# Strict triangle and partial products of a triangular substitution held in PSUM, corner products on other PSUM banks

## The chip, the core and the metric

The kernel runs on one core of a Trainium2 chip, in one launch. The metric is the device time of one execution in microseconds (us). The kernel before has a median of 1243.59 us over three runs (1241.88 to 1249.92). Engine names are those of the profile: PE is the matrix engine (PEld its weight loads), DVE the vector engine, ACT the scalar engine, POOL the GpSimd engine, SP the engine that issues most DMAs. SBUF is the large on-chip memory; PSUM is the small one that PE writes, eight banks of 512 float32 numbers in each of 128 partitions.

## The reference

256 tokens of width 1024 pass through a block of attention, retention, cross attention and a mixture of experts, and then through a second block of two layers. The second layer of that block opens with a "time mix" of 16 heads of width 64, and only its recurrence concerns the change:

```
def _rwkv7_step(state, inp):
    r_t, w_t, k_t, v_t, a_t, b_t = inp
    sa = jnp.einsum('bhvk,bhk->bhv', state, a_t)
    state = (state * w_t[:, :, None, :] + sa[..., None] * b_t[:, :, None, :]
             + v_t[..., None] * k_t[:, :, None, :])
    return state, jnp.einsum('bhvk,bhk->bhv', state, r_t)
```

Each head's state takes a rank-one correction in every one of the 256 steps. The result then passes a group norm, a gate and the product with `w_o`, and a feed-forward part ends the layer.

## The kernel before

The kernel goes through the phases A to G in turn. Phase F is the time mix (`phase_f`), G the feed-forward part behind it. The code is written in one order; a scheduler sets, engine by engine, the order in which the instructions stand, and each engine then works its queue strictly in that order, waiting on semaphores.

Phase F cuts the 256 steps into four chunks of 64. Inside a chunk the corrections form a unit lower triangular system for each head, and the kernel inverts it. 4 chunks x 16 heads give 64 triangles of 64 x 64. Each is split into two diagonal triangles of 32 x 32 and a corner. The 128 small triangles lie one to a partition.

- **The triangles.** PE forms the products `ar` x `kb`; ACT copies the diagonal blocks into the tile `Lc`; DVE transposes `Lc` into `Ll` (L1757), after which each partition holds one strict triangle as 32 x 32 numbers.
- **The substitution.** A loop of 31 steps (L1758 in the source; its instructions are recorded under the helper line L329): step `s` multiplies column `s` of `Ll` below the diagonal by row `s` of the growing inverse `Xl` into a temporary tile from the ring `s` (seven buffers in this phase), and adds that to `Xl`. That is 62 DVE instructions of (31-s)(s+1) elements each, every one dependent on the one in front of it.
- **Beside it.** The table `BETWEEN["substitution"]` names the steps that are written next to the loop, in order: `v` (second half of the value projection), `c` (`corners`: PE forms the corner products, ACT copies them to `Lo`), `p` (`products`: the 128 x 128 products of chunks 0 to 3; ACT copies them into the tiles `G`, called `k` in the trace, and POOL masks them, L1786), `g` (`gate`, whose second operand POOL splits, L364), `t` (`turned`: PE transposes keys into `BK`).
- **PSUM.** Two pools of four banks each: `psa` (tiles `acc`) and `psb` (tiles `ps`). The value projection, `products`, `turned` and `gate` take `acc`; the triangles, `corners` and the steps behind the substitution take `ps`.
- **Behind it.** DVE transposes `Xl` back into `XC` (the buffer `Lc`, L1839) and into `YC` (L1840). `merge` computes the corner of the inverse on PE in two rounds with DVE copies between them (`P1`, then `X`); ACT copies the diagonal parts from `Lc` into `X`.
- **POOL.** It multiplies the values by `bon` into the tiles `gb` (L1886, eight instructions; `gb` is allocated from the ring `s`), fetches `rowF` in four DMAs (L1894), clears `R` (L1889), and later folds the gate into `gb` and `gt`.
- **The chunk loop.** For each chunk, PE forms `pr`, ACT copies it to `R` (L1943), PE multiplies `R` by `X` (`ps<-R,X`), ACT copies the result to `UV` (L1950), and PE forms outputs and the new state. `normed` runs the group norm: 16 ACT instructions `s<-acc,gnb,gr` for the first two chunks. `lin_res` multiplies by `w_o`, part of which lies split in `held`.

Of the kernel before, what the change touches and what calls it, by code (L numbers as in the profile page):

```python
# [15 lines left out]
ALU = mybir.AluOpType  # L16
# [3 lines left out]
P = 128  # L20
# [189 lines left out]
class Block:  # L210
# [1249 lines left out]
    def phase_f(self, x, with_ffn):  # L1460
        nc = self.nc
# [25 lines left out]
        for b in range(4):  # L1487
# [6 lines left out]
            s = slice(2 * b, 2 * b + 2)  # L1494
# [61 lines left out]
        pr = [self.psa(512) for _ in range(4)]  # L1556
# [171 lines left out]
        def run(spec):  # L1728
            for k in spec:
                next(steps[k], None)  # L1730
# [6 lines left out]
        Lc, Lo, Ll, Xl = (k32(n) for n in ("Lc", "Lo", "Ll", "Xl"))  # L1737
# [6 lines left out]
        for p in range(2):  # L1744
            pl = [self.psb(512).rearrange("p (n x) -> p n x", n=8) for _ in range(2)]
# [4 lines left out]
            for hh in range(2):  # L1750
# [3 lines left out]
                        self.act(Lc[r, 16 * p + hh : 16 * p + 16 : 2, :], pl[hh][r, :, 32 * b : 32 * b + 32])  # L1754
                run(BETWEEN["removals"][2 * p + hh])

        nc.vector.transpose(Ll, Lc.rearrange("p n t -> p t n"))  # L1757
        for s in range(31):  # L1758
            n, m = 31 - s, s + 1
            pr = self.s2(n * m).rearrange("p (a b) -> p a b", a=n)  # L1760
            self.tt(pr, Ll[:, m:, s : s + 1].broadcast_to([P, n, m]), Xl[:, s : s + 1, 0:m].broadcast_to([P, n, m]), ALU.mult)
            self.tt(Xl[:, m:, 0:m], Xl[:, m:, 0:m], pr, ALU.add)

        G = []
# [52 lines left out]
                    yield  # L1817

        def corners():
            pl = [self.psb(512).rearrange("p (n s) -> p n s", n=16) for _ in range(2)]  # L1820
            r = [slice(Us(q).start + 32, Us(q).start + 64) for q in range(2)]
            for p in range(2):
                for i in range(8):
                    for q in range(2):
                        for ps, rh in zip(pl, halves):
                            self.mm(ps[r[q], 8 * p + i, :], ar[rh, i, 2 * p + q, 0, 32:64], bT(rh, i, 2 * p + q)[:, 0:32], True, True)
            for hh in range(2):
                for q in range(2):
                    self.act(Lo[r[q], hh::2, :], pl[hh][r[q]])
            yield  # L1830

        steps["c"] = corners()
        steps["p"] = chain.from_iterable(products(c) for c in range(4))
        steps["t"] = chain.from_iterable(turned(c) for c in range(3))
# [74 lines left out]
        pr, pu = [self.psb(512) for _ in range(2)], [self.psb(512) for _ in range(2)]  # L1909
# [26 lines left out]
        for c in range(4):  # L1936
            p, q = c // 2, c % 2
# [230 lines left out]
```

## Time and profile before

| | |
|---|---|
| median of three runs | 1243.59 us |
| the profiled execution | 1244.74 us |
| its span, first to last instruction | 1242.9 us |
| busy share of the span: PE, DVE, ACT, POOL | 90%, 58%, 46%, 17% |
| mean granted TensorE clock | 0.957 |
| span part in which phase F's substitution stands | about 914 to 964 us |

The profile is one execution recorded by the hardware. A timeline row gives the start in us from the span's start, the duration, engine, line, operation, what it writes and reads by tile name (buffer numbers left out), a count, and in brackets how long the engine stood idle before it and on whom. Rows of one kind may be merged, and their duration is then that of the stretch. [...] Busy shares over the whole span mix stages with different limits, so a stage is read from its own stretch.

### The profile page before, as it was taken

How to read it: one execution, taken by the hardware profiler on the slowest of the kernel's cores; microseconds unless marked ns; L12 is line 12 of the kernel's file. 1: busy time of each engine (PE TensorE's matmuls, PEld its weight loads, DVE VectorE, ACT ScalarE, POOL GpSimd, SP SyncE). 2: the span in 40 equal slices, each digit the busy share in tenths (PEclk: the TensorE clock that was granted, in tenths of full speed). 3: DMA queues.
4: the chain of work that ended last, by engine and by line, in shares of the span. 5: the costliest groups of instructions: out<-in, count | busy, mean ns of one | idle time of the engine just before them, and what ended most of it. 6: DMA issues, size and time to landing. Idle time of an engine off the chain costs nothing. (4 is left out here: it accounts for less than half of the span.)

```text
span 1242.9 us, 18727 instructions
## 1 busy us (share of the span) xinstructions
PE 1121.5 (90%) x7070; PEld 869.8 (70%) x7070; DVE 725.4 (58%) x1332; ACT 574.0 (46%) x1114; POOL 217.3 (17%) x192
## 2 busy tenths in 40 slices
PE   6999999979888868999999999579993988999998
PEld 5778878734333316878888887578972977888887
DVE  4978565531111106765766665986679646766665
ACT  5667555310000005675545544457772344555452
POOL 2101000000000011200000000786575820100000
PEclk9999999979999979999999999897997798999999
DMA  8543595899999985633766664133411205766662
GB/s 279 169 118 116 177 395 189 296 349 409 409 409 409 409 346 174 170 119 119 223 186 188 192 192 127 40 84 103 151 41 35 69 18 169 214 190 190 187 187 68
DMA packets 125154, 246.04 MB, mean 198 GB/s; under 512 B 11666, under 2 KB 66354, under 8 KB 125059
## 3 DMA queue, kind: packets, MB, share of 16 engines
q1 hardware_dynamic: 123250, 240.52, 57.8%
q0 software_dynamic: 1520, 4.01, 1.1%
q8 instruction: 57, 0.93, 0.3%
q10 hardware_dynamic: 288, 0.26, 0.1%
q14 instruction: 39, 0.31, 0.1%
HBM read 243.70 MB, written 1.05 MB: 197 GB/s over the span
## 5 line engine op out<-in xcount | busy, mean ns | idle before, releaser
L364 DVE TENSOR_TENSOR ws<-w,ws 128x1024 fp32r<-128x1024 f32 (+5 forms) x341 | 327.1, 973 | 161.9 <-ACT ws L363 161.0
L363 ACT CAST ws<-w 128x1024 fp32r<-128x1024 f32 (+6 forms) x365 | 288.3, 805 | 219.3 <-issue 83.3
L312 PE MATMUL ps<-fp,ws 128*128 128x512 f32 (+1 forms) x1472 | 253.8, 333 | 0.2
L312 PEld LDWEIGHTS ps<-fp,ws 128*128 128x128 f32 x1472 | 220.7, 189 | 31.3 <-DVE fp L187 0.6
L312 PE MATMUL acc<-ws,f 128*128 128x512 f32 (+1 forms) x696 | 175.2, 404 | 11.9 <-ACT ws L363 9.3
L312 PEld LDWEIGHTS acc<-ws,f 128*128 128x128 f32 x696 | 131.2, 193 | 41.3 <-ACT ws L363 11.3
L326 ACT ACTIVATE s<-ps 128x256 f32<-128x256 f32 (+2 forms) x114 | 47.0, 414 | 220.7 <-PE ps L312 220.6
L312 PE MATMUL acc<-ws,h 128*128 128x512 f32 x528 | 124.1, 391 | 0.0
L312 PEld LDWEIGHTS acc<-ws,h 128*128 128x128 f32 x528 | 97.7, 188 | 21.0
L312 PE MATMUL acc<-f,ws 128*128 128x256 f32 x480 | 69.9, 301 | 18.2 <-DVE ws L364 11.4
L312 PE MATMUL ps<-we,xs 128*32 128x512 f32 x512 | 76.7, 605 | 3.2 <-DMA we<-in_experts_dram 1.8
L312 PEld LDWEIGHTS acc<-f,ws 128*128 128x128 f32 x480 | 64.5, 204 | 21.3 <-DVE ws L364 13.3
L347 POOL TENSOR_TENSOR rs_r<-rs_v,mhalf 128x2 f32<-128x2 f32 (+3 forms) x26 | 24.4, 944 | 298.6 <-DVE kan L338 180.3
L1112 DVE TENSOR_TENSOR xs<-ps,cols 128x256 f32<-128x256 f32 x32 | 13.6, 424 | 101.8 <-PE ps L312 101.7
L312 PE MATMUL acc<-ws,o 128*128 128x512 f32 x192 | 48.0, 405 | 1.3 <-ACT ws L363 1.2
L312 PEld LDWEIGHTS ps<-Pm,x 128*128 128x128 f32 x256 | 31.9, 198 | 23.1 <-issue 18.8
L312 PE MATMUL acc<-ws,mf 128*128 128x512 f32 x192 | 48.0, 399 | 0.0
L329 DVE TENSOR_TENSOR s<-ps,s 128x256 f32<-128x256 f32 x80 | 33.5, 420 | 24.8 <-ACT s L326 24.8
L312 PE MATMUL ps<-we,hT 128*32 128x512 f32 x256 | 38.6, 663 | 10.2 <-DMA rowD<-in_rowD_dram 6.6
L312 PEld LDWEIGHTS ps<-we,xs 128*32 128x32 f32 x512 | 15.6, 109 | 41.4 <-issue 26.9
L312 PEld LDWEIGHTS acc<-ws,o 128*128 128x128 f32 x192 | 36.4, 194 | 10.0 <-ACT ws L363 1.6
L312 PEld LDWEIGHTS acc<-ws,mf 128*128 128x128 f32 x192 | 35.2, 188 | 6.9
(405 smaller groups left out, 1470.7 us busy)
## 6 DMA issues: line engine op xcount, KB each, us to landing
we<-in_experts_dram SPq DMA_DIRECT2D x192, 512.0 KB, 10.2
w<-in_ffn_w_gate_dram SPq DMA_DIRECT2D x44, 512.0 KB, 4.4
w<-in_ffn_w_up_dram SPq DMA_DIRECT2D x44, 512.0 KB, 4.0
w<-in_ffn_w_down_dram SPq DMA_DIRECT2D x44, 512.0 KB, 3.7
w<-in_hy_w_in_dram SPq DMA_DIRECT2D x20, 512.0 KB, 3.9
w<-in_w_in_dram SPq DMA_DIRECT2D x16, 512.0 KB, 4.5
w<-in_cross_w_kv_dram SPq DMA_DIRECT2D x16, 512.0 KB, 4.1
w<-in_rw_w_o_dram SPq DMA_DIRECT2D x10, 512.0 KB, 3.6
```

Of the source, the lines that this page charges most:

```text
L312: return self.nc.tensor.matmul(out, lhsT, rhs, start=start, stop=stop, skip_group_check=True)
L326: self.nc.scalar.activation(out, in_, func, **kw)
L329: self.nc.vector.tensor_tensor(out, a, b, op)
L347: self.rooted = self.nc.gpsimd.tensor_tensor(r, v, self.mhalf[:, :n], ALU.pow).ins
L363: i = self.nc.scalar.copy(a, src)
L364: j = (sub or self.nc.vector).tensor_tensor(b, src, a.bitcast(F32), ALU.subtract)
L1112: return nc.vector.tensor_tensor(xs[:, 2 * b : 2 * b + 2, :], ps.rearrange("p (k c) -> p k c", k=2), gb, ALU.mult)
```

## The change

The strict triangle is copied after the transpose from `Ll` into two PSUM tiles `Lp` (ACT, 128 x 512 each: columns 0 to 15 and 16 to 31), and the loop reads it there. The products go to one PSUM tile `pr2`, to its two halves in turn, and no longer to the ring `s`. Every instruction of the loop then has one operand in SBUF and one in PSUM. The three tiles come from `psb`; `corners` takes its two banks from `psa` in exchange. The arithmetic is the same.

```
         nc.vector.transpose(Ll, Lc.rearrange("p n t -> p t n"))
+        Lp = [self.psb(512).rearrange("p (t s) -> p t s", t=32) for _ in range(2)]
+        for h in range(2):
+            nc.scalar.copy(Lp[h], Ll[:, :, 16 * h : 16 * h + 16])
+        pr2 = self.psb(512)
         for s in range(31):
             n, m = 31 - s, s + 1
-            pr = self.s2(n * m).rearrange("p (a b) -> p a b", a=n)
-            self.tt(pr, Ll[:, m:, s : s + 1].broadcast_to([P, n, m]), Xl[:, s : s + 1, 0:m].broadcast_to([P, n, m]), ALU.mult)
+            at = s % 2 * 256
+            pr = pr2[:, at : at + n * m].rearrange("p (a b) -> p a b", a=n)
+            self.tt(pr, Lp[s // 16][:, m:, s % 16 : s % 16 + 1].broadcast_to([P, n, m]), Xl[:, s : s + 1, 0:m].broadcast_to([P, n, m]), ALU.mult)
             self.tt(Xl[:, m:, 0:m], Xl[:, m:, 0:m], pr, ALU.add)
...
         def corners():
-            pl = [self.psb(512).rearrange("p (n s) -> p n s", n=16) for _ in range(2)]
+            pl = [self.psa(512).rearrange("p (n s) -> p n s", n=16) for _ in range(2)]
```

The scheduler then sets other orders from this place to the end of phase F. Lines behind the loop move down by six (L1786 becomes L1792, L1886 L1892, L1889 L1895).

**POOL, beside the substitution.** Before: the splits of the gate's operand (`ws`), the masks of chunk 0 (`k_1963`) and chunk 1 (`k_1990`), splits of `w_o`, and only then the eight `bon` products into `gb`.

```order
L364 TENSOR_TENSOR ws_8557<-w_8550,ws_8556 128x512
L364 TENSOR_TENSOR ws_8563<-w_8560,ws_8562 32x512
L1786 TENSOR_TENSOR k_1963_8526<-k_1963_8526,c_gmask 64x16x64
L1786 TENSOR_TENSOR k_1963_8526<-k_1963_8526,c_gmask 128x16x64
L364 TENSOR_TENSOR ws_8567<-w_8560,ws_8566 32x512
L1786 TENSOR_TENSOR k_1990_8632<-k_1990_8632,c_gmask 64x16x64
L1786 TENSOR_TENSOR k_1990_8632<-k_1990_8632,c_gmask 128x16x64
L364 TENSOR_TENSOR ws_9498<-w_9495,ws_9497 128x512
L364 TENSOR_TENSOR ws_9502<-w_9495,ws_9501 128x512
L1886 TENSOR_TENSOR s_2013_8878<-k_1786_7619,bon 64x512 x2
```

In the changed kernel two `bon` products already stand further up, and the other six and three DMAs stand ahead of the gate's last splits and of the mask of chunk 0 (`k_1935`):

```order
L364 TENSOR_TENSOR ws_8531<-w_8524,ws_8530 128x512
L1892 TENSOR_TENSOR s_1986_8853<-k_1786_7619,bon 64x512
L1892 TENSOR_TENSOR s_1987_8854<-UV_7620,bon 64x512
L1892 TENSOR_TENSOR s_1987_8854<-UV_7621,bon 64x512
L1892 TENSOR_TENSOR s_1986_8853<-k_1786_7619,bon 64x512
L1892 TENSOR_TENSOR s_1988_8855<-UV_7620,bon 64x512
L1900 DMA s_1991_8868<-in_rowF_dram 128x512
L1900 DMA s_1992_8869<-in_rowF_dram 128x512
L1900 DMA s_1993_8878<-in_rowF_dram 128x512
L1892 TENSOR_TENSOR s_1988_8855<-UV_7621,bon 64x512
L364 TENSOR_TENSOR ws_8537<-w_8534,ws_8536 32x512
L1792 TENSOR_TENSOR k_1935_8500<-k_1935_8500,c_gmask 64x16x64
```

So a split that PE waits for (`ws_8537`, and after the mask `ws_8541`) moved behind nine instructions. Further down the same queue:

```order
L364 TENSOR_TENSOR ws_8541<-w_8534,ws_8540 32x512
L364 TENSOR_TENSOR ws_9472<-w_9469,ws_9471 128x512
L364 TENSOR_TENSOR ws_9476<-w_9469,ws_9475 128x512
L1792 TENSOR_TENSOR k_1962_8606<-k_1962_8606,c_gmask 64x16x64
L1792 TENSOR_TENSOR k_1962_8606<-k_1962_8606,c_gmask 128x16x64
L364 TENSOR_TENSOR ws_9488<-w_9485,ws_9487 128x512
L1792 TENSOR_TENSOR k_1969_8650<-k_1969_8650,c_gmask 64x16x64
L1792 TENSOR_TENSOR k_1969_8650<-k_1969_8650,c_gmask 128x16x64
L1895 MEMSET R_8864 64x1024
```

The masks of chunk 1 (`k_1962`) and chunk 2 (`k_1969`) stand ahead of the clearing of `R`, which before came ahead of chunk 2's mask.

**ACT, at the end of the substitution.** Before: the last copies of `G` for chunk 2 (`k_1997`) and of `BK`, and then the copies of the inverse's diagonal from `Lc` into `X`.

```order
L326 ACTIVATE k_1997_8676<-acc_8693 64x4x64
L326 ACTIVATE k_1997_8676<-acc_8693 128x4x64
L326 ACTIVATE BK_8381<-acc_8706 128x512
L326 ACTIVATE BK_8381<-acc_8995 128x512
L326 ACTIVATE X_8715<-Lc_8145 32x16x32
L1868 COPY X_8715<-Lc_8145 32x16x32
```

Now, where chunk 1's copies (`k_1962`) are half done:

```order
L326 ACTIVATE k_1962_8606<-acc_8609 128x4x64
L326 ACTIVATE X_8689<-Lc_8145 32x16x32
L1874 COPY X_8689<-Lc_8145 32x16x32
L326 ACTIVATE X_8689<-Lc_8145 32x16x32
L1874 COPY X_8689<-Lc_8145 32x16x32
L326 ACTIVATE X_8690<-Lc_8145 32x16x32
L1874 COPY X_8690<-Lc_8145 32x16x32
L326 ACTIVATE X_8690<-Lc_8145 32x16x32
L1874 COPY X_8690<-Lc_8145 32x16x32
L326 ACTIVATE k_1962_8606<-acc_8622 64x4x64
L326 ACTIVATE k_1962_8606<-acc_8622 128x4x64
```

The eight copies into `X`, which wait for the substitution, moved ahead of the rest of chunk 1, all of chunk 2 and four copies of `BK`.

**PE, at the first round of `merge`** (`ps<-Lc,Lo`). Before, it stands behind all products of chunks 0 to 2:

```order
L323 MATMUL acc_8706<-base,kb_7624 128x128 x4
L323 MATMUL acc_8995<-base,kb_7624 128x128 x4
L312 MATMUL acc_9023<-ar,kb_7624 128x128 x4
L312 MATMUL acc_9024<-ar,kb_7624 128x128 x4
L312 MATMUL ps_8721<-Lc_8145,Lo_8146 32x32 x32
L312 MATMUL ps_8756<-Lc_8145,Lo_8146 32x32 x32
```

Now it stands in the middle of them (`acc_8590` is the gate, `acc_8623` chunk 1, `acc_8652` chunk 2, `base` the transposes into `BK`):

```order
L312 MATMUL acc_8590<-ws_8540,lo_8521 128x512
L312 MATMUL acc_8623<-ar,kb_7624 128x128 x4
L312 MATMUL ps_8695<-Lc_8145,Lo_8146 32x32 x24
L323 MATMUL acc_8636<-base,kb_7624 128x128 x4
L312 MATMUL ps_8695<-Lc_8145,Lo_8146 32x32 x8
L312 MATMUL ps_8730<-Lc_8145,Lo_8146 32x32 x4
L323 MATMUL acc_8642<-base,kb_7624 128x128 x4
L312 MATMUL acc_8652<-ar,kb_7624 128x128 x4
```

The first round of `merge` moved ahead of chunk 2's products and of three transposes.

## Rows read from the trace of the kernel before

**Rows 1.** Timeline of PE: start us, us, engine, line, operation, count [idle before]
```profile
934.02 1.20 PE L312 MATMUL acc<-ws,lo 32*128 32x512 f32 x4
935.15 1.16 PE L312 MATMUL acc<-ar,kb 64*128 64x128 f32 x8
...
964.48 3.47 PE L312 MATMUL ps<-Lc,Lo 32*32 32x32 f32 x122 [21.47 <-DVE Lc L1839]
...
976.73 0.27 PE L312 MATMUL ps<-R,X 128*64 128x64 f32 x1
...
1015.22 2.34 PE L312 MATMUL acc<-held,f 128*128 128x512 f32 x9
...
1018.56 1.14 PE L312 MATMUL acc<-S,ar 64*64 64x64 f32 x16
```

**Rows 2.** Timeline of DVE, the substitution and the transpose behind it
```profile
916.15 1.17 DVE L329 TENSOR_TENSOR s<-Ll,Xl 128x31 f32<-128x31 f32 x1
...
917.67 0.22 DVE L329 TENSOR_TENSOR s<-Ll,Xl 128x60 f32<-128x60 f32 x1
...
925.34 6.11 DVE L329 TENSOR_TENSOR s<-Ll,Xl 128x207 f32<-128x207 f32 x1
...
946.00 0.42 DVE L329 TENSOR_TENSOR s<-Ll,Xl 128x252 f32<-128x252 f32 x1
946.45 0.42 DVE L329 TENSOR_TENSOR Xl<-Xl,s 128x252 f32<-128x252 f32 x1
...
962.51 1.92 DVE L1839 STREAM_TRANSPOSE Lc<-Xl 128x1024 f32<-128x1024 f32 x1
```

**Rows 3.** Timeline of POOL in the same stretch
```profile
926.51 4.71 POOL L1786 TENSOR_TENSOR k<-k,c_gmask 64x1024 f32<-64x1024 f32 x2
931.19 1.39 POOL L364 TENSOR_TENSOR ws<-w,ws 32x512 fp32r<-32x512 f32 x1
...
957.34 4.35 POOL L1886 TENSOR_TENSOR s<-UV,bon 64x512 f32<-64x512 f32 x4
961.63 1.24 POOL L1894 DMA_DIRECT2D s<-in_rowF_dram  x2
962.91 0.94 POOL L1889 MEMSET R<- 64x1024 f32 x1
```

**Rows 4.** Groups by shape, DVE, 971 to 1020: busy us, mean ns | idle
```profile
L1967 DVE TENSOR_TENSOR S<-S,Dc 64x512 f32<-64x512 f32 x4 | 5.1, 1264 | 0.1
...
L329 DVE TENSOR_TENSOR S<-ps,S 64x512 f32<-64x512 f32 x4 | 2.8, 688 | 4.9 <-PE ps L312 4.9
```

**Rows 5.** Stretches: length, busy us by engine, PEclk, DMA share, GB/s
```profile
980.00:990.00 10.00, 10.00 (x183) 9.62 (x182) 6.42 (x9) 4.12 (x6) 9.61 (x7) 1.00 0.24 73
945.00:946.00 1.00, 0.00 (x0) 0.00 (x0) 0.90 (x4) 0.00 (x0) 0.00 (x0) 0.50 0.39 31
976.00:977.00 1.00, 1.00 (x24) 1.00 (x22) 0.00 (x0) 0.00 (x0) 1.00 (x2) 1.00 0.00 0
```

**Rows 6.** Groups by shape, DVE, 700 to 860, columns as in rows 4
```profile
L332 DVE SCALAR_TENSOR_TENSOR x<-acc,rx,x 128x512 f32<-128x512 f32 x4 | 3.0, 750 | 5.3 <-PE acc L312 5.1
L329 DVE TENSOR_TENSOR s<-s,rb 128x512 f32<-128x512 f32 x4 | 2.8, 692 | 0.1
```

**Rows 7.** Timeline of ACT
```profile
915.16 2.40 ACT L326 ACTIVATE Lo<-ps 32x512 f32<-32x512 f32 x4
...
921.46 1.86 ACT L326 ACTIVATE k<-acc 64x256 f32<-64x256 f32 x4 [0.38 <-PE acc L312]
...
964.46 0.63 ACT L326 ACTIVATE X<-Lc 32x512 f32<-32x512 f32 x1 [22.23 <-DVE Lc L1839]
...
998.36 4.85 ACT L326 ACTIVATE s<-acc,gnb,gr 128x64 f32<-128x64 f32 x16 [0.19 <-issue]
1003.24 0.58 ACT L1950 COPY UV<-ps 64x512 f32<-64x512 f32 x1
1006.75 0.58 ACT L1943 COPY R<-ps 64x512 f32<-64x512 f32 x1 [2.94 <-PE ps L312]
```

## The prediction

> **What bounds the kernel now.** I read the page's 40 slices first: PE is busy nearly everywhere, with a hole near 950 us, in phase F. Then the waits of PE: the longest of the program ends there. PE does nothing for 21.5 us until DVE has transposed the finished inverse, and ACT stands for 22.2 us at the same point [rows 1, 7]. So for these 20 us DVE alone sets the time, and the timeline of DVE was read next. The substitution begins at 916.15 and the transpose behind it at 962.51 [rows 2]: 62 instructions in 46.3 us without a gap. An instruction of 252 elements takes 0.42 us there, but one of 207 takes 6.11. That one begins at 925.34 and ends at 931.45; POOL's masks run from 926.51 to 931.22 [rows 3]. Last the groups by shape, in a later stretch where POOL works too (9.61 of 10 us in 980 to 990) [rows 5]: the 512-wide product with both operands in SBUF takes 1264 ns in the mean, the 512-wide sum with one operand in PSUM 688 [rows 4]. The same two-operand work is thus slowed beside POOL when both operands lie in SBUF, and not when one lies in PSUM. The change gives all 62 instructions a PSUM operand.
>
> **The substitution itself.** Two undisturbed durations, 0.22 us for 60 elements and 0.42 for 252, give 1.04 ns an element and 0.157 us fixed; two neighbours start 0.45 us apart, so about 0.035 lies between them [rows 2]. The sum of (31-s)(s+1) over 31 steps is 5,456, twice that 10,912 elements: 11.4 us. 62 x 0.157 = 9.7, 62 x 0.035 = 2.2. Together 23.3 us instead of 46.3: 23.0 us were contention.
>
> That takes PSUM to cost what SBUF costs. Reading it does: 688 ns [rows 4] against 692 for two SBUF operands with no POOL beside them [rows 6]. Writing PSUM from DVE, and reading it back in the next instruction, no row shows. The nearest rows are these two, 4 ns cheaper, and the dearest 512-wide arithmetic row with a PSUM operand, 750 ns, 58 above 692 [rows 6]. Over 62 instructions: 0.2 us less to 3.6 us more. I take zero, the row nearest in kind.
>
> [...]
>
> **What is added in front.** ACT copies the triangle in two instructions. A copy of this kind takes at most 0.63 us [rows 7]. The loop needs the first alone: it begins at about 916.9 instead of 916.15, ends at 916.9 + 23.3 = 940.2, and with 1.92 us for the transpose [rows 2] PE and ACT could go on at 942.1, 22.4 us earlier than 964.48.
>
> But these copies wait for the transpose at 916.1 in ACT's queue, and behind them stand a cast and the corner copies, which began at 915.16 [rows 7]. Two copies end at 917.4, the cast at 918.0: what follows on ACT is 2.8 us later, POOL's splits and chunk 0's products (which now need the corner's banks) with it. As to SP, its queue keeps its order.
>
> **What is late next: POOL.** The second half of the values left PSUM at 923.3 (end of the four at 921.46, two of chunk 0 and two of values [rows 7]); now 926.1. For this the moved `bon` products wait. Behind the wait on POOL stand six of them at 1.09 us, three DMA issues at 0.62, the split `ws` at 1.39 [rows 3]: 6.5 + 1.9 + 1.4 = 9.8, so 935.9. Then chunk 0's mask 4.7 and the last split 1.4: 942.0. PE waits for this split in its queue, then has four matmuls (1.20) and a tile of products (1.16) [rows 1] ahead of `merge`: 944.4. So 20.1 us of the 22.4 are left at the first matmul of `merge`. The two `bon` products further up fill a gap on POOL and cost nothing; without that gap they would cost 2.2.
>
> **And behind `merge`, work that before was done.** ACT makes eight copies into `X` first: 942.1 + 8 x 0.63 = 947.2. Eight further copies and casts, at 0.47 (four in 1.86) to 0.63 each [rows 7] 3.8 to 5.0 us, finish chunk 1; I take 4.1: 951.3. POOL then masks chunk 1 (4.7), splits (1.4), masks chunk 2 (4.7) and clears `R` (0.94) [rows 3]: 963.0. ACT has eleven pieces left for chunk 2's mask, 5.2 us, done at 956.5, ahead of POOL's need at 957.4. PE cannot multiply `R` by `X` before `R` is cleared: 963.1 instead of 976.73 [rows 1]. That is **13.6 us** earlier. POOL, not DVE, is late next, and keeps 8.8 of the 22.4 us.
>
> **From there to the last output.** Before, the second `UV` copy of chunk 2 stood behind 16 group-norm instructions of 4.85 us, and the next copy to `R` came at 1006.75 [rows 7]. Now it goes ahead (0.6 us), the 16 follow, and `R` can be copied at 998.4 + 0.6 + 4.85 = 1003.8: **2.9 us** gained (0 if PE is not ready, 5 at most by the second copy). Nine `held` matmuls (2.34 us) stood between the two halves of the last outputs and now stand behind them; since the first half's norm is as late as the second's, I count **1.2** of it (0 to 2.3).
>
> **PE's clock.** [...] Now PE has shorter holes: about 4 us while it waits for the gate's split, and one near 945 while ACT copies `X`. If these bring the clock down, eight tiles of products (four of chunk 1, four of chunk 2, 1.16 each) take up to twice as long, at most 9.3 us more, of which POOL and ACT, just as late, hide a third or more: 0 to 6. I take **3.0** as a loss.
>
> **Sum.** 13.6 + 2.9 + 1.2 - 3.0 = 14.7 us. The profiled execution took 1244.74 us, 1.84 more than its span; 1244.74 - 14.7 = 1230.0. It stands 1.15 above the median of the runs shown (1243.59), so **1229 us** is forecast as the median. What follows phase F keeps its order but for small swaps and is fed by DMAs that free buffers start; I take it to move as a whole.
>
> **Rivals.**
> 1. *The whole gap closes.* POOL and ACT make up for their new order, and phase F shifts by the 22.4 us: 1221. For it: POOL has no DVE to share with. Against it: the order puts both masks ahead of the clearing of `R`, and 4.7 + 1.4 + 4.7 + 0.9 us follow a copy that ACT makes after `X`.
> 2. *PSUM is dear for DVE.* 58 ns [rows 6] for each of 62 instructions on the path: 3.6 us, 1232.6. For it: no row of DVE writing PSUM. Against it: 688 against 692. [...]
> 3. *Contention is not lifted.* The 62 instructions keep their 46.3 us, and the copy in front adds 0.75: about 1244.3. For it: rows 4 compare a sum with a product. Against it: both do the same work per element, and the long instructions of the loop coincide with POOL's.
> 4. *The round trip through PSUM stalls: slower.* In 31 pairs DVE reads in PSUM what it wrote one instruction before. If the read waits beyond the 0.035 us between neighbours, it decides from 14.7 / 31 = 0.47 us a pair on; at 0.75 us a pair, 23 us, the gain turns into a loss of 8.6, and the time is 1252. For it: no row shows the pair. Against it: SBUF pairs of the same dependence run at 0.45 us.
>
> **Chances.** Forecast 0.57, rival 1 0.12, rival 2 0.18, rival 3 0.07, rival 4 0.06. A measurement of this kernel tells about 1% (12.4 us) from no change, so faster means below 1231.2. Around 1229 about three quarters of the forecast's 0.57 lie below it, with rival 1 and a little of rival 2: 0.59. Rival 4 at its price is slower by 0.7% and only beyond it over 1%: 0.04. The rest, 0.37, is within 1%. The range takes the bounds of the terms: best 13.6 + 5 + 2.3 - 0 + 0.2 = 21.1, 1222.5; worst 13.6 - 6 - 3.6 = 4.0, 1239.6. Little lies at the far ends: 1221, to take in rival 1, to 1238.
>
> **What would show it.** In the profile of the changed kernel: no instruction of the loop over 0.5 us, and about 23 us from its first to the transpose; `merge` near 944, with PE idle in two shorter holes; POOL clearing `R` near 963 and `ps<-R,X` right behind it; the `UV` copy of chunk 2 ahead of the 16. The prediction is wrong if loop instructions still stretch beside POOL (rival 3), if all are longer by the same amount (2, or 4 where only the sums are), or if `R` is cleared well away from 963.

## The result, and the profile after

| | before | after |
|---|---|---|
| median of six runs each | 1247.56 us (1241.88 to 1249.92) | 1233.31 us (1232.04 to 1236.21) |
| the profiled execution | 1244.74 us | 1233.26 us |
| its span | 1242.9 us | 1231.5 us |

The ratio is 0.9885, with a 95% interval of 0.9864 to 0.9907: 1.15% faster, about 14 us. Before's profiled execution was 2.8 us quicker than its median, so the two traces differ by 11.5 us only. Of these, 0.9 come from ahead of the change: the transpose into `Ll` begins at 913.11 instead of 914.00. All positions below are therefore counted from the start of that transpose.

**The loop.** DVE, grouped by line and names, 915 to 942 (columns as in [rows 4]; the mean runs over all shapes):

```profile
L329 DVE TENSOR_TENSOR ps<-ps,Xl 128x31 f32<-128x31 f32 (+15 forms) x31 | 10.8, 349 | 1.8 <-ACT ps L1761 0.7
L329 DVE TENSOR_TENSOR Xl<-Xl,ps 128x31 f32<-128x31 f32 (+15 forms) x31 | 10.5, 339 | 1.1
```

Timeline of DVE after, to be held against [rows 2]:

```profile
913.11 2.06 DVE L1758 STREAM_TRANSPOSE Ll<-Lc 128x1024 f32<-128x1024 f32 x1 [7.90 <-ACT Lc L326]
915.83 0.20 DVE L329 TENSOR_TENSOR ps<-ps,Xl 128x31 f32<-128x31 f32 x1 [0.66 <-ACT ps L1761]
...
925.29 0.43 DVE L329 TENSOR_TENSOR ps<-ps,Xl 128x252 f32<-128x252 f32 x1
925.75 0.42 DVE L329 TENSOR_TENSOR Xl<-Xl,ps 128x252 f32<-128x252 f32 x1
...
933.47 0.38 DVE L329 TENSOR_TENSOR ps<-ps,Xl 128x207 f32<-128x207 f32 x1
...
939.38 1.93 DVE L1845 STREAM_TRANSPOSE Lc<-Xl 128x1024 f32<-128x1024 f32 x1
```

The first product starts at 915.83, the transpose at 939.38: 23.5 us instead of 46.3. No instruction is longer than 0.43 us. With 252 elements the product, which writes PSUM, takes 0.43 and the sum 0.42, as in SBUF. At 933.47 POOL is in the middle of a mask, as the next rows show, and DVE takes 0.38 us for 207 elements. POOL's work did not move out of the loop's way: POOL is busy for 20.0 of the loop's 23.4 us (before, for 29.3 of 46.4).

Timeline of POOL after (in [rows 3] before):

```profile
931.87 1.25 POOL L364 TENSOR_TENSOR ws<-w,ws 32x512 fp32r<-32x512 f32 x1
933.10 4.69 POOL L1792 TENSOR_TENSOR k<-k,c_gmask 64x1024 f32<-64x1024 f32 x2
937.75 1.25 POOL L364 TENSOR_TENSOR ws<-w,ws 32x512 fp32r<-32x512 f32 x1
...
961.03 1.95 POOL L1895 MEMSET R<- 64x1024 f32 x2
```

**Behind the loop.** Timeline of PE after, against [rows 1]:

```profile
933.18 2.07 PE L312 MATMUL acc<-ws,lo 32*128 32x512 f32 x4 [2.79 <-POOL ws L364]
...
943.16 2.07 PE L312 MATMUL acc<-ar,kb 64*128 64x128 f32 x8
945.16 1.49 PE L312 MATMUL ps<-Lc,Lo 32*32 32x32 f32 x48
...
964.93 1.90 PE L312 MATMUL ps<-R,X 128*64 128x64 f32 x29
...
986.76 0.97 PE L312 MATMUL ps<-R,X 128*64 128x64 f32 x13
...
1004.22 1.14 PE L312 MATMUL acc<-S,ar 64*64 64x64 f32 x16
1005.29 3.01 PE L312 MATMUL acc<-held,f 128*128 128x512 f32 x12
...
1016.10 4.18 PE L312 MATMUL acc<-ws,f 128*128 128x512 f32 x8 [4.29 <-DVE ws L364]
...
1026.72 8.56 PE L312 MATMUL acc<-ws,f 128*128 128x512 f32 x37
```

Stretches of the span after (columns as in [rows 5]; PEclk is the clock granted to PE as a share of full speed):

```profile
930.00:935.00 5.00, 2.21 (x5) 1.22 (x5) 4.62 (x12) 0.57 (x1) 4.86 (x5) 0.74 0.47 157
935.00:940.00 5.00, 5.00 (x25) 4.35 (x25) 4.49 (x16) 2.62 (x7) 4.01 (x3) 0.50 0.00 0
...
950.00:955.00 5.00, 5.00 (x34) 4.67 (x34) 0.36 (x1) 2.74 (x8) 4.84 (x3) 0.50 0.30 105
955.00:960.00 5.00, 4.53 (x191) 4.05 (x191) 2.74 (x5) 1.73 (x6) 5.00 (x4) 0.84 0.02 5
```

The wait of 21.47 us in front of `merge` is gone, and a wait of 2.79 us for POOL's split stands in its place, earlier. From 933 to 956 PE works with no wait over 0.6 us, but at a granted clock of 0.50: eight chunk products take 2.07 us, where [rows 1] has 1.16. POOL has cleared the first half of `R` at about 962.0 (half of 1.95 behind 961.03). PE forms `ps<-R,X` only at 964.93, behind work of its own.

Where the time was gained and given back, from five starts in the two traces, each counted from the start of the transpose:

| start of | before | after | earlier by |
|---|---|---|---|
| transpose back, `Lc<-Xl` (DVE) | 48.5 | 26.3 | 22.2 |
| `merge`, first matmul | 50.5 | 32.1 | 18.4 |
| `ps<-R,X`, chunk 0 | 62.7 | 51.8 | 10.9 |
| last outputs, `acc<-S` | 104.6 | 91.1 | 13.4 |
| the 37 matmuls `acc<-ws,f` behind the norm | 124.2 | 113.6 | 10.6 |

The end of the span keeps these 10.6. Three rows of before that stand in no group ahead carry the last line and the term on `UV` below. Timeline of PE before (996.08 is chunk 2; in after it is 986.76):

```profile
996.08 0.97 PE L312 MATMUL ps<-R,X 128*64 128x64 f32 x13
...
1038.20 8.55 PE L312 MATMUL acc<-ws,f 128*128 128x512 f32 x37
```

Timeline of ACT before, and behind it that of after (its first row is to be held against 921.46 in [rows 7]):

```profile
1009.48 0.58 ACT L1943 COPY R<-ps 64x512 f32<-64x512 f32 x1 [2.15 <-PE ps L312]
```

```profile
922.01 1.88 ACT L326 ACTIVATE k<-acc 64x256 f32<-64x256 f32 x4 [0.35 <-PE acc L312]
...
990.29 4.85 ACT L326 ACTIVATE s<-acc,gnb,gr 128x64 f32<-128x64 f32 x16
...
995.89 0.58 ACT L1949 COPY R<-ps 64x512 f32<-64x512 f32 x1 [0.34 <-PE ps L312]
```

### The profile page after: what moved, and what is told of

The parts are those of the page before. It is cut to its first block, busy times and chain, and to the rows that moved or that the text cites. A ratio compares the mean times of both kernels' runs of the same rounds, so it can differ in the third digit from the quotient of the medians.

```text
span 1231.5 us, 18724 instructions
## 1 busy us (share of the span) xinstructions
PE 1127.2 (92%) x7070; PEld 874.4 (71%) x7070; DVE 703.1 (57%) x1332; ACT 574.8 (47%) x1116; POOL 219.8 (18%) x192
## 3 DMA queue, kind: packets, MB, share of 16 engines
q1 hardware_dynamic: 123250, 240.52, 56.6%
## 5 line engine op out<-in xcount | busy, mean ns | idle before, releaser
L312 PE MATMUL acc<-ws,f 128*128 128x512 f32 (+1 forms) x696 | 177.5, 408 | 13.6 <-ACT ws L363 7.4
L312 PE MATMUL acc<-ws,h 128*128 128x512 f32 x528 | 124.1, 391 | 0.0
L312 PEld LDWEIGHTS acc<-f,ws 128*128 128x128 f32 x480 | 65.6, 207 | 19.7 <-DVE ws L364 12.1
L1112 DVE TENSOR_TENSOR xs<-ps,cols 128x256 f32<-128x256 f32 x32 | 13.6, 425 | 101.6 <-PE ps L312 101.5
L312 PE MATMUL ps<-we,hT 128*32 128x512 f32 x256 | 36.9, 622 | 10.5 <-DMA rowD<-in_rowD_dram 6.7
L312 PEld LDWEIGHTS ps<-we,xs 128*32 128x32 f32 x512 | 15.6, 110 | 42.0 <-issue 25.9
L347 POOL TENSOR_TENSOR rx<-rs_v,mhalf 128x2 f32<-128x2 f32 x6 | 7.3, 1208 | 191.9 <-DVE rs_v L338 106.3
```

The lines of the kernel that those rows point to most:

```text
L312: return self.nc.tensor.matmul(out, lhsT, rhs, start=start, stop=stop, skip_group_check=True)
L347: self.rooted = self.nc.gpsimd.tensor_tensor(r, v, self.mhalf[:, :n], ALU.pow).ins
L1112: return nc.vector.tensor_tensor(xs[:, 2 * b : 2 * b + 2, :], ps.rearrange("p (k c) -> p k c", k=2), gb, ALU.mult)
```

## The experiments

The theory, drawn from the 6.11 us of a product of 207 elements through POOL's masks [rows 2, 3] and the 0.38 us of one of 207 elements in the middle of a mask in after: an instruction on DVE whose inputs both lie in SBUF stands still while POOL works, and one PSUM input lifts that. The gain is then partly kept back by the order that the scheduler makes of the rest. Rivals: the gain comes with the exchange of banks; POOL's work merely stands beside the loop no longer; POOL's clearing of `R` is what is late next (the prediction's view). The table gives all runs, counted as above; each position is from one profiled execution, each ratio from timed runs.

| run | loop to transpose back | `R,X` chunk 0 | last outputs | 37 matmuls | median us | ratio to before |
|---|---|---|---|---|---|---|
| before | 48.5 | 62.7 | 104.6 | 124.2 | | |
| after | 26.3 | 51.8 | 91.1 | 113.6 | 1233.31 | 0.9885 (0.9864 to 0.9907) |
| e1_banks | 48.5 | 62.7 | 104.5 | 124.1 | 1248.60 | 0.9993 (0.9974 to 1.0012) |
| e2_triangle | 43.1 | 56.6 | 95.9 | 118.4 | 1239.48 | 0.9928 (0.9900 to 0.9957) |
| e3_products | 36.2 | 62.8 | 101.9 | 124.4 | 1245.58 | 0.9975 (0.9956 to 0.9994) |
| e8_mask2 | 53.5 | 67.9 | 106.8 | 129.7 | 1252.48, one run | |
| e4_bon_behind | 26.3 | 45.1 | 87.0 | 109.5 | 1231.42 | 0.9858 (0.9829 to 0.9888) |
| e5_x_behind | 26.3 | 52.6 | 91.8 | 114.5 | 1238.11 | 0.9912 (0.9886 to 0.9939) |
| e6_tail | 26.3 | 48.4 | 87.1 | 108.8 | 1231.68 | 0.9857 (0.9829 to 0.9885) |
| e7_late | 26.2 | 46.7 | 87.7 | 109.7 | 1230.32 | 0.9850 (0.9822 to 0.9878) |
| e10_late_again | 26.3 | 40.1 | 86.7 | 108.8 | 1229.78 | 0.9855 (0.9819 to 0.9890) |
| e11_after_again | 26.3 | 49.5 | 88.7 | 111.2 | 1233.40 | 0.9875 (0.9842 to 0.9908) |
| e9_fill | 26.3 | 44.0 | 89.2 | 110.6 | 1232.81 | 0.9857 (0.9823 to 0.9892) |
| e12_cast | 26.3 | 44.5 | 85.6 | 107.7 | 1230.61 | 0.9869 (0.9847 to 0.9890) |

### Which part of the change lifts the contention

**e1_banks**, the bank exchange alone, on the kernel before:

```
-            pl = [self.psb(512).rearrange("p (n s) -> p n s", n=16) for _ in range(2)]
+            pl = [self.psa(512).rearrange("p (n s) -> p n s", n=16) for _ in range(2)]
```

> The kernel before with one edit: the corner products take their two banks from the pool acc instead of ps; the loop stays in SBUF. Theory (contention of two-SBUF-operand work on DVE with POOL): the loop still takes 42 to 48 us with some 20 instructions over 1 us, and the time is that of before, 1240 to 1250 us. Rival (the bank exchange and the order it brings are the gain): phase F is shorter without the PSUM operands, 1236 us or less.

The loop and every later position stayed within 0.1 us of before, and the ratio includes 1. The rival falls.

**e2_triangle**, the changed kernel with the products in the SBUF ring:

```
-            pr = pr2[:, at : at + n * m].rearrange("p (a b) -> p a b", a=n)
+            pr = self.s2(n * m).rearrange("p (a b) -> p a b", a=n)
```

> The changed kernel with the products back in the SBUF ring: only the triangle lies in PSUM, so the 31 products read one PSUM operand and the 31 sums have all operands in SBUF. Theory: only the sums wait for POOL, none of the products exceeds 0.5 us; the loop takes 31 to 39 us (23.5 plus about half of the 23 lost before), the time is 1236 to 1246 us. Rival (every operand has to leave SBUF, or the lock does not go by instruction): the loop takes over 42 us and the time is that of before. Other rival (POOL's work merely fell beside the loop in the changed kernel): the loop takes about 24 us, 1233 us.

**e3_products**, the changed kernel with the triangle in SBUF (no copies `Lp`):

```
-            self.tt(pr, Lp[s // 16][:, m:, s % 16 : s % 16 + 1].broadcast_to([P, n, m]), Xl[...], ALU.mult)
+            self.tt(pr, Ll[:, m:, s : s + 1].broadcast_to([P, n, m]), Xl[...], ALU.mult)
```

> The changed kernel with the triangle left in SBUF: only the products lie in PSUM, so the 31 sums read one PSUM operand, and the 31 products read two SBUF operands and write PSUM. Theory with inputs deciding: the products wait for POOL (over 1 us where POOL works), the sums do not; loop 31 to 39 us, time 1236 to 1246. Theory with any PSUM operand deciding, the output too: no instruction over 0.5 us, loop 23 to 24 us, and without the two copies in front the time is 1 us below the changed kernel's, about 1232.

Groups of DVE, e2, 915 to 962:

```profile
L329 DVE TENSOR_TENSOR Xl<-Xl,s 128x31 f32<-128x31 f32 (+15 forms) x31 | 27.4, 883 | 1.1
L329 DVE TENSOR_TENSOR s<-ps,Xl 128x31 f32<-128x31 f32 (+15 forms) x31 | 10.6, 341 | 2.0 <-ACT ps L1761 0.7
```

The same of e3:

```profile
L329 DVE TENSOR_TENSOR ps<-Ll,Xl 128x31 f32<-128x31 f32 (+15 forms) x31 | 21.3, 688 | 1.1
L329 DVE TENSOR_TENSOR Xl<-Xl,ps 128x31 f32<-128x31 f32 (+15 forms) x31 | 10.5, 339 | 1.1
```

Whatever reads a PSUM operand lies at the means of after (341 and 339 ns, there 349 and 339); whatever reads two SBUF operands is stretched (883 and 688). In e3 the products write PSUM and are stretched all the same: the inputs decide, not the output. So each half of the change frees one half of the instructions, and both are needed.

e2's loop was longer than expected, 40.4 us from its first product at 917.17 to the transpose at 957.53 (expected 31 to 39), because a single sum stood for 5.70 us through both masks; its time lay in the range. e3 was expected at 1236 to 1246 and came at 1245.58, hardly below before, although its loop is 12.4 us shorter. Timeline of ACT, e3:

```profile
951.25 0.63 ACT L326 ACTIVATE X<-Lc 32x512 f32<-32x512 f32 x1 [12.13 <-DVE Lc L1842]
...
956.32 0.77 ACT L326 ACTIVATE k<-acc 64x256 f32<-64x256 f32 x2
```

The scheduler had set the copies into `X` ahead of the rest of chunk 1, as in after. Here the loop ends 10 us later than there; ACT stands 12.13 us at the first of these copies, chunk 1 and chunk 2 wait behind them, and `R,X` is no earlier than before. A shorter loop is worth only what the order behind it lets through.

**e8_mask2**, the kernel before with chunk 0's 0/1 mask applied twice on POOL:

```
+                for _ in range(2 if c == 0 else 1):
                     nc.gpsimd.tensor_tensor(G[c][r, :, cs_], G[c][r, :, cs_], m..., ALU.mult)
```

> The kernel before with one suspected cost doubled: POOL multiplies chunk 0 by its 0/1 mask twice, which leaves the numbers as they are and adds 4.7 us of POOL work beside the loop. Theory (a DVE instruction with all operands in SBUF stands until POOL's running instructions end): one or two instructions of the loop absorb the whole addition, such as 6.1 becoming 10 to 11 us, the loop grows from 46.3 to about 51 us, and the time by 3 to 5 us. Rival (the long instructions are slow for a reason of their own, such as the DMA or a shape): the 46.3 us stay.

Timeline of DVE, e8, and behind it that of POOL:

```profile
927.63 11.98 DVE L329 TENSOR_TENSOR s<-Ll,Xl 128x207 f32<-128x207 f32 x1
```

```profile
927.56 1.28 POOL L364 TENSOR_TENSOR ws<-w,ws 32x512 fp32r<-32x512 f32 x1 [3.14 <-ACT ws L363]
928.80 4.71 POOL L1787 TENSOR_TENSOR k<-k,c_gmask 64x1024 f32<-64x1024 f32 x2
933.48 1.26 POOL L364 TENSOR_TENSOR ws<-w,ws 32x512 fp32r<-32x512 f32 x1
934.71 9.57 POOL L1787 TENSOR_TENSOR k<-k,c_gmask 64x1024 f32<-64x1024 f32 x4
```

The instruction of 207 elements that took 6.11 us in [rows 2] now takes 11.98: it stood from 927.63 to 939.61, through a split, two mask instructions, another split and half of the four that follow. The loop grew by 4.9 us, as expected. The long instructions are POOL's doing. What this costs the whole program is not shown: the one run, 1252.48 us, lies within the spread of before in its job (1245.93 to 1253.27).

### What keeps part of the gain

**e4_bon_behind**: the eight `bon` products queue on POOL behind chunk 1's mask, where they stood before.

```
+                    with self.behind(masked[1]):
                         pool(h8(gb[p][hb][Ks(q)]), h8(UV[2 * p + q]...), bq, ALU.mult)
```

> The changed kernel with the eight bon products on POOL queued behind the mask of chunk 1, where they stood before the change; everything else is the scheduler's. Theory (POOL's new order, by the late split of the gate's operand, makes PE wait, its clock fall and chunk products run at half speed, and thus keeps part of the 22.9 us that the loop gave): PE has no wait of 2 us or more ahead of merge, the clock stays at 1.00 up to 940, R,X of chunk 0 starts at 956 to 960 instead of 964.9, and the time is 1225 to 1229. Rival (PE's clock would have fallen anyway, and the copies into X on ACT set the end): R,X at 963 or later and the time within 2 us of the changed kernel's.

The split that PE waits for comes 20.0 us behind the transpose's start in after and 14.0 in e4, PE's wait of 2.79 us is gone, and `R,X` comes 6.7 us earlier; the last outputs keep 4.1 of it. The median is 1.9 us below after's, less than expected, and the clock fell at 939.1 although PE had no wait over 0.2 us in the 15 us before. So POOL's order is not all that brings the clock down. That it costs something is likely, but not shown. The ratios' intervals overlap (0.9829 to 0.9888 and 0.9864 to 0.9907), and with one order `R,X` moves with PE's clock from one execution to the next: e6 below has e4's orders up to there, its clock was 0.50 in every stretch from 940 to 960, where e4's was 1.00 from 950 to 956, and `R,X` came at 48.4 against 45.1; the second trace of after's kernel, e11, has 1.00 from 955 to 960, where after has 0.84, and 49.5 against 51.8. (The positions expected in the trace's own time, 956 to 960 for `R,X`, were missed: this trace's loop stands 3.2 us later, and `R,X` came at 961.5.)

**e5_x_behind**: after, with the eight copies into `X` behind chunk 2's copies on ACT.

```
-        with self.behind(self.moved):
+        with self.behind(self.moved, self.turned):
             for p, q, ns, b0, b1 in places:
```

> The changed kernel with one order edit on ACT: the eight copies of the inverse's diagonal into X queue behind the copies of chunk 1, chunk 2 and BK. Theory (in the changed kernel these eight copies, 5.1 us, stand in front of the copies that free PE's acc banks, and so hold chunk 2's products and the second half of merge): ACT copies chunk 1 from 941.5 instead of 946.4, the second half of merge comes 2 to 4 us earlier than 955.9, R,X of chunk 0 at 961 to 962.5, and the time is 1229 to 1231 us. Rival (POOL's masks ahead of the clearing of R set the point, as the prediction had it): R,X stays behind the clearing of R, within 1 us of 964.9 when counted from the start of the loop, and the time is that of the changed kernel within 1 us.

Neither side held. The copies of chunk 1 went ahead as wanted, but `merge`'s second half and `R,X` did not move (52.6 against 51.8), and the time rose to 1238.11. Timeline of POOL, e5, then of PE:

```profile
959.94 1.94 POOL L1895 MEMSET R<- 64x1024 f32 x2
```

```profile
936.98 5.01 PE L312 MATMUL acc<-ar,kb 64*128 64x128 f32 x24
...
966.78 1.90 PE L312 MATMUL ps<-R,X 128*64 128x64 f32 x29
```

`R` is cleared for chunk 0 at about 960.9, 46.7 us behind the start, and `R,X` begins 5.9 us after that. Neither POOL nor ACT is late there, but PE, whose rows follow each other with no wait over 0.5 us at the low clock, 0.50 from 935 to 955 (24 chunk products in 5.01 us). The median rose by 5 us while the profiled trace ends only 1.9 us later than after's; that trace is the quickest of the five runs (1235.19 to 1241.68), and what the slower ones lose was not found.

**e7_late** and, the same kernel in another job, **e10_late_again**: e4, with the second half of chunk 2's products and its transposes written into the chunk loop. **e11_after_again** is the changed kernel itself.

```
-    substitution="vcvvpgpggtgtppgttppt",
-    chunks=(("", "", "tt"), ("p", "p", ""), ("", "", ""), ("", "", "")),
+    substitution="vcvvpgpggtgtppgttp",
+    chunks=(("p", "t", "tt"), ("p", "p", ""), ("", "", ""), ("", "", "")),
```

> The kernel with the bon products behind the mask of chunk 1, and the second half of chunk 2's products and its transposes written behind the loop (next to chunk 0's outputs) instead of beside it; the scheduler then clears R before it masks chunk 1. Theory (chunk 2's part of the queue on ACT and POOL is what now stands ahead of R,X): R,X of chunk 0 begins 1 to 3 us earlier against the loop's start than with the bon edit alone (there 45.1 us behind the start of the first transpose), and the time is 1229 to 1231. Rival (PE's products at the half clock set it, and they are as many as before): within 1 us of 1231.4.

> The kernel with the bon edit and chunk 2 behind the loop once more, with more rounds beside the changed kernel: theory (POOL's order and PE's clock keep part of the gain in the changed kernel) 2 to 4 us below the changed kernel in the same job; rival (a difference between jobs): within 1 us of it.

> The changed kernel itself, unaltered, on the same chip and in the same job: 1232 to 1235 us, and 0.986 to 0.990 of before.

Both times the time lay as expected, 3.0 us and 3.6 us under after's. The positions expected of e7 were missed: `R,X` came at 46.7, behind e4's 45.1 and not 1 to 3 us ahead of it, so the time came out right for another reason than the one given. That e7 is faster than e4 (1230.32 against 1231.42, in two jobs) is not shown either. The two executions recorded have one instruction order and two clocks. Timeline of PE, e7:

```profile
935.59 2.07 PE L312 MATMUL acc<-ar,kb 64*128 64x128 f32 x8
...
949.47 3.46 PE L312 MATMUL ps<-Lc,Lo 32*32 32x32 f32 x122
...
959.70 0.92 PE L312 MATMUL ps<-R,X 128*64 128x64 f32 x13
```

Timeline of PE, e10:

```profile
937.18 1.16 PE L312 MATMUL acc<-ar,kb 64*128 64x128 f32 x8
...
944.97 2.19 PE L312 MATMUL ps<-Lc,Lo 32*32 32x32 f32 x123
...
954.58 1.49 PE L312 MATMUL ps<-R,X 128*64 128x64 f32 x13
```

Stretches of e10, those of e7 behind them:

```profile
940.00:945.00 5.00, 5.00 (x54) 4.59 (x54) 4.48 (x6) 4.95 (x14) 4.92 (x4) 1.00 0.02 3
945.00:950.00 5.00, 4.36 (x229) 4.13 (x230) 3.64 (x6) 4.41 (x8) 4.77 (x5) 0.90 0.01 3
```

```profile
930.00:935.00 5.00, 4.89 (x33) 3.76 (x32) 4.59 (x13) 2.55 (x7) 3.77 (x3) 1.00 0.16 51
935.00:940.00 5.00, 5.00 (x21) 4.04 (x20) 4.52 (x15) 3.33 (x8) 1.78 (x1) 0.55 0.14 54
```

In e7 the clock fell near 935.5 though PE had been busy for 4.89 of the 5 us from 930 to 935; in e10 it stayed at 1.00 until about 949, behind a wait of 0.41 us at 947.67. With the clock up, `R,X` comes 6.6 us earlier (40.1 against 46.7). This is what the low clock costs PE here. Yet the last outputs come only 1.0 us earlier. Timeline of ACT, e10:

```profile
965.78 0.62 ACT L363 CAST ws<-w 128x512 fp32r<-128x512 f32 x1 [7.41 <-DMA w<-in_rw_w_o_dram]
966.43 1.06 ACT L1951 COPY R<-ps 64x512 f32<-64x512 f32 x2
```

ACT stands 7.41 us at a cast of `w_o` for its DMA, and the next copies to `R` queue behind it. In e7, where PE comes later, the same cast waits only 2.12 us and begins at much the same place (52.0 us behind the start, here 51.3). So a third engine, waiting for a transfer, takes over as soon as PE is early.

**e9_fill**: e7, with 12 repeated matmuls on PE in the gate, to hold the clock.

```
-                    for b in range(2):
+                    for b in (0, 0, 1):
                         self.mm3(po, ..., b == 0, b == 1)
```

> The kernel with the bon edit and chunk 2 written behind the loop, plus idle work on PE: the first three matmuls of each of the gate's four tiles are done twice (12 matmuls of 128 rows and 512 columns, about 0.25 us each, 3 us in all; the second set starts the sum anew, so the numbers stay). Theory (what now stands ahead of R,X is PE's own work, 24 us without a wait at the granted clock 0.50, and the clock fell in a stretch where PE had only short, thin work): with the added work the clock stays at 1.00 beyond 940, the 32 products of chunk 2 take about 3.1 us instead of 5.1, R,X of chunk 0 comes 2 to 5 us earlier against the loop's start, and the time is 1226 to 1229 us in spite of the 3 us of work. Rival (the clock falls all the same): R,X 1 to 3 us later, the time 1231 to 1234.

The clock did stay at 1.00, to about 954 (0.95 in the mean of 950 to 955, 0.50 behind it), and chunk 2's 32 products took 3.08 us. `R,X` came 2.7 us earlier than e7's, within what was expected, but later than e10's; the scheduler also set eight chunk products into the middle of `merge` here (at 956.48). The time, 1232.81, missed its range and lies in the rival's. As e10 kept the clock without the extra work, this run does not show that the work held it. No gain shows.

**e12_cast**: e7, with the casts of `w_o` behind chunk 1's copies to `R`.

```
+            with self.behind(copied):
                 self.lin_res(o, I["w_o"], x, None, ((1, (0,), None),))
```

> The kernel with the bon edit and chunk 2 behind the loop, and one more order edit on ACT: the casts of the w_o pieces for the first output product queue behind chunk 1's copies to R. Theory (with R,X of chunk 0 as early as 40 us behind the loop's start, the last outputs still come 86.7 us behind it, because ACT stands 7.4 us at such a cast for the DMA of w, and chunk 1's copies to R queue behind it): that wait goes, the last outputs come 83 to 85.5 us behind the start, and the time is 1226 to 1229 us against the 1229.8 to 1230.3 of the kernel without this edit. Rival (chunk 2's mask on POOL or the transfers for the gate set the end anyway): the last outputs at 86.5 or later, the time 1229 to 1231.

The last outputs came at 85.6, the earliest of all, but just past the upper bound of what was expected, and the median did not move (1230.61). The chain of waits then ran through POOL's `bon` products, mask and `rowF` sums: much as the rival has it, though the last outputs came ahead of its 86.5.

**e6_tail**: e4, with DVE's splits of `w_o` no longer behind the norm's last sum (`self.behind(self.z_done)` becomes `self.behind()`).

> The kernel with the bon products behind the mask of chunk 1, and one more order edit: the splits of w_o on DVE in the last product no longer queue behind the group norm's last sum. Theory (of the gain at the last outputs some 3 us are given back because DVE's splits stand behind the norm, so that PE waits 4.3 us): that wait falls below 2 us, and the time lies 1.5 to 3 us below the 1231.4 of the kernel without this edit. Rival (the transposes of the norm's result are late anyway, and the matmuls moved forward only fill a wait of the same length further on): no gain, 1231 to 1232.

Timeline of PE, e6, in place of the wait of 4.29 us that after has at 1016.10 and e4, just as long, at 1015.24:

```profile
1013.53 0.49 PE L312 MATMUL acc<-ws,f 128*128 128x512 f32 x1 [1.73 <-ACT ws L363]
1015.36 2.90 PE L312 MATMUL acc<-ws,f 128*128 128x512 f32 x5 [1.33 <-DVE ws L364]
...
1025.29 8.55 PE L312 MATMUL acc<-ws,f 128*128 128x512 f32 x37
```

The wait of 4.29 became two of 1.73 and 1.33, the 37 matmuls came 0.7 us earlier than in e4, and the median did not move: the rival.

## Why the prediction was right, and where not

The forecast was 1229 us (1221 to 1238), faster by over 1% with 0.59. Measured: 1233.31 and, in a second job, 1233.40; 1.15% faster, with an interval that reaches from 0.93 to 1.36%. The time lies inside the range, and the direction and its cause hold. Behind the loop, errors of several steps cancel, which was luck. By its steps:

1. **The loop, 46.3 to 23.3 us: right.** 23.5. The halves e2 and e3 (883 and 688 ns in the mean with two SBUF inputs, 341 and 339 with one) and the doubling in e8 (4.9 us more) show that it was contention with POOL.
2. **Writing PSUM costs nothing: right, to about 10 ns.** The products, which read and write PSUM, take 0.20, 0.31, 0.38 and 0.43 us at 31, 135, 207 and 252 elements; before's undisturbed ones, in SBUF alone, take 0.19, 0.30, 0.37 and 0.42. The sums are no longer than before's: 0.37 at 207 elements and 0.42 at 252 in both. Rivals 2, 3 and 4 fall with this.
3. **In front: right. ACT's delay of 2.8: only at first.** Transpose to first product took 2.72 us instead of 2.15, and the transpose back ended 28.2 us behind the start, as forecast (942.1 less 914.0 is 28.1). ACT's corner copies began 2.6 us later (916.89), but the four copies of values and chunk 0 only 1.4 (922.01, against 921.46 before), since before's ACT had stood 1.07 us for PE in between, and the delay went into that wait.
4. **POOL up to the last split: too slow by 2 us.** Forecast 28.0 behind the start, measured 25.9 (939.0); the six `bon` products had begun at 10.6 (923.75), not at 12.1. `merge` came all the same 1.7 us later than forecast (32.1 against 30.4). PE at the low clock (0.50) still had 24 chunk products in front of it and took the split only at 941.16; the four matmuls and eight products behind that took 2.07 each, not 1.20 and 1.16.
5. **`R` cleared at 963.0 (49.0 behind the start): right, and not what decided.** Measured about 48.9. The step that failed here is "POOL, not DVE, is late next". PE was later: it came to `R,X` at 51.8. e5 had `R` cleared earlier, and `R,X` did not move. In e11 the two nearly meet, `R` cleared at 48.9 and `R,X` at 49.5. In e10, which clears `R` early too (27.6), PE at the high clock (1.00 until about 949) came to `R,X` at 40.1.
6. **The clock, 3.0 us (0 to 6): a good size for the wrong place.** Its "up to twice as long" rests on [rows 5]: 0.50 at 945 to 946, with PE idle since 943.0, and 1.00 at 976 to 977. The forecast added it to POOL's time; in fact PE at the low clock replaced POOL as the last. `R,X` was 2.7 us behind the forecast without it, 0.4 in e11, where the clock was back at 1.00 by 955. That 13.6 less 3.0, 10.6, met the 10.9 measured was luck. Of the two holes forecast for PE one came, 2.79 us at the gate's split; near 945 PE waited 0.58. What the forecast left out is that before pays for the clock as well: it is at 0.50 from 964 to 975 there, and the first round of `merge` takes 3.47 us [rows 1], where e10's, at 1.00, takes 2.19.
7. **The `UV` copy, 2.9: larger, and partly paid for before.** From `R,X` of chunk 0 to that of chunk 2, 2.5 us were lost again (8.4 us earlier at 986.76, before 996.08); from there to chunk 3's second copy to `R`, 4.3 were won (1009.48 less 996.08 is 13.4; 995.89 less 986.76 is 9.1).
8. **"What follows phase F keeps its order ... I take it to move as a whole", and 1.2 for the `held` matmuls: the terms that failed.** The nine matmuls of 2.34 us left the gap between the outputs, and stand behind the outputs now (1005.29). The last outputs came 13.4 us earlier, near the 14.7 of the sum, but the 37 matmuls behind the norm only 10.6. Between these two places PE now has the nine matmuls, 2.3 us of work, in addition, and its waits there sum to 4.6 us, 4.29 of them for a split that DVE makes behind the norm; before had 3.2 us of waits there, in four places. So what the shift of the `held` matmuls took out ahead of the last outputs came back behind them. By the positions the sum is 10.9 - 2.5 + 4.3 + 0.7 (to the last outputs) - 2.9 = 10.5, where 14.7 was forecast.

So by the positions the forecast was 4 us too good, nearly all by step 8. Between the medians lie 14.2 us, close to the 14.6 forecast, and this is luck as well: the forecast started from 1243.59, the median of three runs of before, and that of six is 1247.56. That the medians lie 14 to 17 us apart and the traces 10.6 and, with e11, 13.0 is explained only in part. In the job of e11 before's runs spread over 10 us, the longest with the lowest mean granted clock (1243.86 at 0.960, 1254.35 at 0.945), after's over 5; only one execution of before was recorded, a quick one.

The lowest medians are those of e7's kernel: 1230.32 and 1229.78, some 3.3 us under the changed kernel. In the job that ran both the ratios to before were 0.9855 and 0.9875, and their intervals overlap, so that this order is faster than the changed kernel's is not shown.

## What to carry to other kernels

Where small dependent instructions on DVE run beside POOL, look for one whose duration is that of POOL's instruction rather than of its own elements (here 6.11 us for 207 elements that alone take 0.37); give each one PSUM input, and check input by input, since here the place of the output did not count (e3's products, which write PSUM from two SBUF inputs, took 688 ns in the mean; e2's, which write SBUF from one, 341). Then read what else was put into the hole: a table of orders, or a scheduler that sets the work anew around a loop of another length, can leave a second and a third engine late next. And check the gain at the end of the part that follows, not at the last instruction of the stage: matmuls that are moved out of a gap still have to be done somewhere in the kernel.

## What the runs showed of the hardware that was not expected

- A DVE instruction that waits for POOL does not always get in between two of POOL's instructions: in e8 one stood for 11.98 us through six of them. Beside the two masks that followed, one got in for each (2.41 and 2.42 us). What decides this was not tried.
- The granted clock fell to 0.50 without an idle stretch of PE in front of it: in e7 from near 935.5, with PE busy for 4.89 of the 5 us from 930 to 935. The same instruction order in e10 kept 1.00 there. A forecast can give the clock a range, not a value.
